# Moving one tap and the history copies of a short convolution from VectorE to ScalarE, in a decoder layer with gated DeltaNet and GLA heads

## The chip, the core and the metric

The kernel runs on one core of one Trainium2 chip. The metric is the device time of one execution in microseconds; for the kernel before, three executions were timed. All arithmetic is float32; large matrix products split each operand into a high and a low part (float32r) and use three matmuls.

## What is computed

One layer of a hybrid decoder for 16 meta tokens, 1024 prompt tokens and 8 samples of 8 tokens. One input projection feeds two groups of heads (gated DeltaNet, "GDN", and GLA); their outputs go through one output projection, a layer norm, a convolutional feed-forward network and a second layer norm. The change lies in the causal convolution of width 4 on the 1536 columns q, k, v of the GDN heads, which follows the projection and comes ahead of a silu:

```python
def causal_conv(x, buf, w):
    width = w.shape[0]
    L = x.shape[1]
    ext = jnp.concatenate([buf.astype(x.dtype), x], axis=1)
    out = ext[:, 0:L] * w[0]
    for i in range(1, width):
        out = out + ext[:, i:i + L] * w[i]
    return out, ext[:, L:]

p = h @ w_in
qkv, new_conv = causal_conv(qkv_pre, conv_buf, gdn_conv_w)
qkv = jax.nn.silu(qkv)
```

The last three rows of the input of each sequence (`new_conv`) are an output too.

## The kernel before

Features lie on the 128 partitions, tokens along the free dimension. There are 1152 positions (48 empty ones, the meta tokens, the prompt, the samples), worked on in three blocks of 384 (`BLK`); the first block leaves out its 48 empty positions in the projections (336 columns).

Phase A, the first half, treats one block after the other. `block(b, order)` emits its parts in the sequence of the string `ORDER[b]`: `k` is the projection, convolution and silu of one of eight feature tiles of q and k, `v` the same for one of four tiles of v, `q`, `V`, `d`, `g` are other projections, `n` norms and the set-up of the GDN heads, `a` and `b` steps of the GLA heads. So `conv_qkv` is called 12 times for each block, 36 times in all. What is emitted is then put in order by a scheduler with its own estimates, engine by engine; instructions of different parts, and of neighbouring blocks, stand mixed on each engine, and each engine works its list strictly in that order. Other work than the convolution may therefore stand elsewhere when the convolution's instructions change.

A projection: SyncE loads 128 x 512 pieces of weights (`wraw`, two for each feature tile), ScalarE copies them to the high part `wwhi` (L212), GpSimd (POOL in the profile) subtracts to get the low part `wwlo` (L213), TensorE does 24 matmuls (L231 to L233) into one of two PSUM banks `mm`. The next projection but one can only start when the bank has been read.

`conv_qkv` then builds the tile `u` (one of two buffers): three history columns, then the block's columns. VectorE copies the history in (L340) and, for blocks 0 and 1, the last three columns out to `hist` for the next block (L345); ScalarE copies the projection from PSUM to `u` (L344). The convolution is four VectorE instructions on `u` into the output tile `o` (named `kq` or `v` in the profile): one product (L371), then three multiply-adds (L373). In block 2 the last 64 columns are the samples, which have a history each; the four taps are done separately for 320 and 64 columns, and L358 and L359 copy the final rows into `ce`, which TensorE turns for the output. ScalarE then makes the sigmoid from three passes (`e`, L329 to L331) and GpSimd multiplies (L375).

Two other stretches matter below. The set-up of the GDN heads inverts a triangular matrix for all chunks by some 60 short dependent VectorE instructions on `lw` and `t` (L558, L560), followed by two transposes (L565, L566); TensorE's L577 needs the first of them. The output projection of blocks 0 and 1 (`out_proj`, matmuls on `mhi` and `mlo`, its sum in `zo` by VectorE at L1111, the low parts `mlo` at L1098) has no dependence on block 2, and the scheduler places it among block 2's work. Phase C, the second half, is the feed-forward network (tiles `up`, `dn`).

Of the kernel before, what the change touches and what calls it, by code (L numbers as in the profile page):

```python
# [46 lines left out]
def hymba_step_kernel(  # L47
# [26 lines left out]
    # tiles in use until the end of the mixers, away from those that the first layer norm's result will cover  # L74
# [3 lines left out]
    def load_x(i):  # L78
        """rows of token tile i (48 empty positions, meta tokens, prompt, samples)."""
# [54 lines left out]
    # ones where two tokens share a chunk (or sample) and the first is not after the second  # L134
# [30 lines left out]
    # per-feature parameters, one row of 128 per feature tile, turned by the tensor engine  # L165
# [44 lines left out]
    def split(raw, hi, lo):  # L210
        """raw = hi + lo, both exact in float32r"""
        act.activation(out=hi, in_=raw, func=AF.Copy)  # L212
        pool.tensor_tensor(out=lo, in0=raw, in1=hi.bitcast(F32), op=ALU.subtract)  # L213

    def stage(src, a, order=(0, 1)):
        """weights [128, a, 1024 / a] as a list of a pairs (hi, lo)"""
        res = {}
        for h in order:
            raw, hi, lo = halves(1, "w")
            v = lambda t: t.rearrange("p (a c) -> p a c", a=a // 2)  # L220
            sp.dma_start(out=v(raw), in_=src[:, h * a // 2:(h + 1) * a // 2])
            split(raw, hi, lo)
            res[h] = [(v(hi)[:, k], v(lo)[:, k]) for k in range(a // 2)]
        return res[0] + res[1]
# [4 lines left out]
    def mm3(ps, lh, rh, first, last):  # L229
        """ps += lh^T rh with both operands as (hi, lo)."""  # L230
# [4 lines left out]
    def layer_norm_rows(small, t, m, src):  # L235
        """t[:m] = (src - mean) * rsqrt(var + eps), rows are tokens; src is a list of two halves."""
# [12 lines left out]
    # =====================================================================  # L249
    # phase A: input projection and both mixers, in three blocks of 384 positions  # L250
    # (48 empty positions, 16 meta tokens, 1024 prompt tokens, 64 sample tokens)
    # =====================================================================
# [23 lines left out]
    def ln_tile(i, hl):  # L276
        """input layer norm of token tile i, turned to features x tokens, to DRAM (and to hi + lo)."""
# [24 lines left out]
    def load_h(b):  # L302
        """normalised input of block b, features x tokens, as hi + lo."""
# [22 lines left out]
    def sigmoid(y, lo=0):  # L326
        """1 / (1 + exp(-y)) = exp(-log(1 + exp(-y)))"""
# [6 lines left out]
    def conv_qkv(b, h, f, o):  # L334
        """projection, causal convolution and silu of feature tile f of q | k | v."""
# [4 lines left out]
        dve.tensor_copy(out=u[:, 0:3], in_=hist[:, f])  # L340
        if b == 0:
            dve.memset(u[:, 3:3 + NPAD], 0.0)
        if b < 2:
            act.activation(out=u[:, 3 + lo:3 + BLK], in_=ps[:, lo:BLK], func=AF.Copy)  # L344
            dve.tensor_copy(out=hist[:, f], in_=u[:, BLK:BLK + 3])  # L345
            parts = [(o, lambda i: u[:, i:i + BLK])]
        else:
# [10 lines left out]
            dve.tensor_copy(out=ce[:, 0:3], in_=u[:, 320:323])  # L358
            dve.tensor_copy(out=ce[:, 3:27].rearrange("p (s i) -> p s i", i=3), in_=us[:, :, 8:11])  # L359
# [9 lines left out]
        tap = lambda i: par[:, TAP + 12 * i + f:TAP + 12 * i + f + 1]  # L369
        for dst, at in parts:  # L370
            dve.tensor_scalar(out=dst, in0=at(0), scalar1=tap(0), scalar2=None, op0=ALU.mult)  # L371
            for i in range(1, 4):
# [18 lines left out]
    def small_in(b, h, out):  # L391
        """decay and step size of the eight GDN heads, tokens on rows; low-rank gate of GLA.

        X: Hb, Hk, Gk, GL - Hk, ln beta, GL of the three token tiles (the first four filled by small_norm)."""
# [17 lines left out]
        # log1p(e) = 2 atanh(e / (2 + e)), e = exp(-|x|)  # L412
# [32 lines left out]
    def small_norm(b, G, X, pss):  # L445
        """norms of k and q folded into the decay exponents, per token and head; rows to DRAM and columns."""
# [18 lines left out]
        # per chunk, the token of head B on partitions 0-63 and that of head A on 64-127  # L465
# [26 lines left out]
    def rms_out(b, hb, po, bank, tmp, tot, scale, g_col, sg, feat):  # L492
        """po (two feature tiles x 192 tokens) normalised per head, gated, written out for the output projection."""
# [14 lines left out]
    def gdn_setup(b, kqs, col, out):  # L508
        """la: decayed k k^T (strict part used) and q k^T of all pairs and chunks, transposed, rows swapped;
        xf: inverses of I + M, M the strict part."""  # L510
# [40 lines left out]
        # column j of the inverse takes the place of column j of -L once that has been used  # L551
# [10 lines left out]
        # xf: X = [[X11, 0], [-X22 M21 X11, X22]] of every chunk, turned  # L562
# [40 lines left out]
    def q_decayed(b, p, kq):  # L603
        """q e^G of pair p, norms folded, in the place of q."""
# [6 lines left out]
    def gdn_batch(b, p, hb, kq, v, col, gln, gls, la, xf, sv, sam, mq):  # L611
        """three chunks of a pair: U's first part into sv, [state | output] operators into mq."""
# [5 lines left out]
        # v and k with tokens on partitions (head B 0-63, head A 64-127)  # L618
# [13 lines left out]
        # w = beta y, (I + M beta) y = [v | e^G k]  # L632
# [13 lines left out]
        # [gl I - Wk^T kd | q e^G - (A Wk)^T]  # L646
# [10 lines left out]
        if s3:  # L657
            for r, ri in halves_:
                pe.matmul(ps[ri, 320:384], wkb[r, 2], la[p][r, 1, 320:384], start=True, stop=True)
            # (in tiles that the previous block's pairs have left)  # L660
# [25 lines left out]
    def gdn_scan(b, g, hb, mqs, sv, sv2, sam, sg):  # L686
        """recurrence over three chunks of two pairs; sv2 takes the next state (None at the end of the block)."""
# [19 lines left out]
        if b == 2 and hb == 1:  # L707
            if g == 0:
                sts = [wk2.tile([128, 8, 64], F32, tag="t2", name="st", bufs=2) for _ in range(4)]
            else:  # L710
                # (in tiles that the GLA heads have left)
# [82 lines left out]
    def mix_gla(b, P, gq, gk, gkl, sgs):  # L794
# [11 lines left out]
        # 16 x the cumulated log decay of each chunk  # L806
# [9 lines left out]
        # k e^{b_last - b}, tokens on partitions  # L816
# [20 lines left out]
        # keys against the end of their 16-block and of their 4-block  # L837
# [18 lines left out]
        def scores(ps, k, n0, n, q):  # L856
            """keys of n chunks against the queries q of each, rows of the two heads swapped."""
# [166 lines left out]
    def block(b, order):  # L1024
        """emits block b; order gives its parts: s small_in, q GLA q and k, V GLA v, k GDN q and k, n norms and
        setup, v GDN v, d GDN gates, g GLA gates, l next block's layer norm, a / b steps of the GLA mixers."""
# [55 lines left out]
    # =====================================================================  # L1082
    # phase B: output projection and first layer norm
    # =====================================================================
    def out_proj(b, zs=None):
        """residual + output projection of block b, features x tokens, to DRAM or to the tile zs."""
# [5 lines left out]
        # the GLA heads are done before the GDN heads  # L1092
# [29 lines left out]
    # per-feature parameters of the FFN: the samples' earlier rows, three taps, bias  # L1122
# [21 lines left out]
    def ln1(i, z=None):  # L1144
        """first layer norm of token tile i, turned to features x tokens as hi + lo."""
# [38 lines left out]
    # =====================================================================  # L1184
    # phase C: convolutional FFN, features on partitions
    # =====================================================================
    # (of the meta tokens only the last two count on, as the convolution's first rows)
# [60 lines left out]
    for j in range(NFF):  # L1248
# [6 lines left out]
        # the sum over two feature blocks goes on between the steps of the next two, and after the last  # L1255
# [7 lines left out]
        if j == 0:  # L1263
            # the banks and the rest of the memory change hands with the first two feature tiles on their way
# [91 lines left out]
```

## Time and profile before

| | us |
|---|---|
| median of three executions | 1785.52 |
| lowest, highest | 1781.99, 1792.48 |
| span of the profiled execution | 1796.3 |
| in it: TensorE busy | 1657.2 (92%) |
| VectorE busy | 1063.3 (59%) |
| GpSimd busy | 873.2 (49%) |
| ScalarE busy | 742.1 (41%) |

The span runs from the first to the last instruction of one profiled execution; no other time of that execution was taken, and its span is 10.8 us above the median of the timed ones. A group row names line, engine, operation, output and inputs, shapes and count; behind the bar stand the busy time of the group in us and the mean duration of one in ns, then the idle time of the engine just ahead of them. In the answers on one line of the code, three numbers are the shortest, median and longest duration in ns. A wait row gives the total in us, the times, and the longest. "Chain" is the work that ended last, followed back from the last instruction to what released it.

### The profile page before, as it was taken

What the parts mean: (1) busy time and instruction counts of PE and PEld (TensorE: products, weight loads), DVE (VectorE), ACT (ScalarE), POOL (GpSimd) and SP (SyncE); (2) the same over time, 40 slices, a digit from 0 to 9 for tenths busy, and PEclk for the clock granted to TensorE, in tenths of its full rate; (3) what the DMA queues carried; (4) which work ended last, traced back from release to release, by engine and by line L of the source; (5) the groups of instructions that cost most, each with busy time, mean ns of one, the idle gap of its engine ahead of it and who ended that gap; (6) DMA issues with size and microseconds to landing.
All of it is one profiled execution on the core that took longest, in us unless ns stands there. A gap on an engine that the chain in (4) does not pass through costs nothing.

```text
span 1796.3 us, 30948 instructions
## 1 busy us (share of the span) xinstructions
PE 1657.2 (92%) x11939; PEld 1521.1 (85%) x11939; DVE 1063.3 (59%) x2083; ACT 742.1 (41%) x1457; POOL 873.2 (49%) x908
## 2 busy tenths in 40 slices
PE   5788799989889998899988999999999999999997
PEld 4677577878677777778878999999999999999996
DVE  7939867696887788962265374443434443434345
ACT  4555544456644556442254433333233323332332
POOL 4756636666555557553354443433334333433336
PEclk9989899989989999798998999999999999999999
DMA  5346313435423224535461111111111111111112
GB/s 147 92 131 164 104 51 89 123 101 136 113 68 89 76 64 117 154 97 139 118 198 42 54 48 42 48 42 48 42 47 44 42 48 42 48 42 48 37 60 100
DMA packets 229504, 148.06 MB, mean 82 GB/s; under 512 B 22251, under 2 KB 222173, under 8 KB 229357
## 3 DMA queue, kind: packets, MB, share of 16 engines
q1 hardware_dynamic: 229357, 146.09, 29.1%
q8 instruction: 94, 1.54, 0.4%
q14 instruction: 53, 0.43, 0.1%
HBM read 124.09 MB, written 21.95 MB: 81 GB/s over the span
## 4 chain that ended last, share of the span: by engine, by line
PE 64%; DVE 19%; DMA 5%; issue 4%; POOL 4%; ACT 3%; SPq 1%; POOLq 0%; ACTq 0%; DVEq 0%
PE up L231 9%; PE up L233 9%; PE up L232 9%; PE dn L233 5%; PE dn L231 5%; PE dn L232 5%; PE mm L232 3%; PE mm L233 3%; PE mm L231 3%; DVE kq L373 2%; DVE lw L560 2%; DVE t L558 2%; DVE qm L886 1%; DVE v L373 1%; DMA mraw<-mixd 1%
## 5 line engine op out<-in xcount | busy, mean ns | idle before, releaser
L213 POOL TENSOR_TENSOR wwlo<-wraw,wwhi 128x512 fp32r<-128x512 f32 x304 | 404.2, 1334 | 520.5 <-ACT wwhi L212 479.9
L212 ACT ACTIVATE wwhi<-wraw 128x512 fp32r<-128x512 f32 x304 | 189.6, 626 | 351.4 <-PE up L232 194.6
L1243 DVE TENSOR_TENSOR acc<-acc,dn 128x364 f32<-128x364 f32 (+1 forms) x216 | 112.3, 531 | 375.7 <-PE dn L233 372.2
L231 PE MATMUL up<-h1hi,wwhi 128*128 128x352 f32 (+2 forms) x1008 | 333.0, 331 | 0.0
L232 PE MATMUL up<-h1lo,wwhi 128*128 128x352 f32 (+2 forms) x1008 | 332.1, 330 | 0.0
L233 PE MATMUL up<-h1hi,wwlo 128*128 128x352 f32 (+2 forms) x1008 | 331.1, 329 | 0.0
L233 PE MATMUL mm<-hhi,wwlo 128*128 128x384 f32 (+1 forms) x576 | 202.5, 353 | 16.6 <-POOL wwlo L213 16.6
L231 PE MATMUL mm<-hhi,wwhi 128*128 128x384 f32 (+1 forms) x576 | 202.2, 351 | 16.7 <-ACT u L344 8.5
L232 PE MATMUL mm<-hlo,wwhi 128*128 128x384 f32 (+1 forms) x576 | 198.3, 344 | 0.0
L232 PEld LDWEIGHTS up<-h1lo,wwhi 128*128 128x128 f32 x1008 | 190.0, 189 | 0.6
L233 PEld LDWEIGHTS up<-h1hi,wwlo 128*128 128x128 f32 x1008 | 189.9, 188 | 0.1
L231 PEld LDWEIGHTS up<-h1hi,wwhi 128*128 128x128 f32 x1008 | 189.6, 188 | 0.2
L232 PE MATMUL dn<-glo,dwh 128*128 128x364 f32 (+1 forms) x480 | 157.4, 328 | 0.0
L231 PE MATMUL dn<-ghi,dwh 128*128 128x364 f32 (+1 forms) x480 | 155.7, 328 | 0.4 <-ACT dwh L212 0.3
L233 PE MATMUL dn<-ghi,dwl 128*128 128x364 f32 (+1 forms) x480 | 151.1, 328 | 0.1
L233 PEld LDWEIGHTS mm<-hhi,wwlo 128*128 128x128 f32 x576 | 112.7, 196 | 27.7 <-POOL wwlo L213 24.3
L231 PEld LDWEIGHTS mm<-hhi,wwhi 128*128 128x128 f32 x576 | 113.5, 197 | 26.1 <-ACT u L344 10.2
L1204 ACT ACTIVATE u<-up 128x352 f32<-128x352 f32 x84 | 38.8, 462 | 194.7 <-PE up L233 193.3
L232 PEld LDWEIGHTS mm<-hlo,wwhi 128*128 128x128 f32 x576 | 113.1, 196 | 2.6 <-issue 1.4
L213 POOL TENSOR_TENSOR dwl<-draw,dwh 128x512 fp32r<-128x512 f32 x40 | 74.5, 1864 | 52.1 <-ACT dwh L212 52.1
L1216 DVE SCALAR_TENSOR_TENSOR y<-u,fpar,y 128x1104 f32<-128x1104 f32 x44 | 94.5, 2148 | 1.1
L231 PEld LDWEIGHTS dn<-ghi,dwh 128*128 128x128 f32 x480 | 90.1, 188 | 0.9 <-ACT dwh L212 0.5
(413 smaller groups left out, 3541.0 us busy)
## 6 DMA issues: line engine op xcount, KB each, us to landing
wraw<-in_w_in_dram SPq DMA_DIRECT2D x168, 256.0 KB
wraw<-in_w_up_dram SPq DMA_DIRECT2D x88, 256.0 KB
wraw<-in_w_out_dram SPq DMA_DIRECT2D x48, 256.0 KB
draw<-in_w_down_dram SPq DMA_DIRECT2D x44, 256.0 KB
hd<-xt SPq DMA_DIRECT2D x9, 512.0 KB
la<-gd SPq DMA_DIRECT2D x24, 192.0 KB
out_dram<-z SPq DMA_DIRECT2D x8, 512.0 KB
xt<-in_x_prompt_dram SPq DMA_DIRECT2D x7, 512.0 KB
```

The lines of the kernel that those rows point to most:

```text
L212: act.activation(out=hi, in_=raw, func=AF.Copy)
L213: pool.tensor_tensor(out=lo, in0=raw, in1=hi.bitcast(F32), op=ALU.subtract)
L231: pe.matmul(ps, lh[0], rh[0], start=first, stop=False)
L232: pe.matmul(ps, lh[0], rh[1], start=False, stop=False)
L233: pe.matmul(ps, lh[1], rh[0], start=False, stop=last)
L373: dve.scalar_tensor_tensor(out=dst, in0=at(i), scalar=tap(i), in1=dst, op0=ALU.mult, op1=ALU.add)
L558: dve.tensor_tensor(out=tv, in0=bc(lw[:, j + 1:32, j:j + 1], 128, n, j), in1=bc(lw[:, j:j + 1, 0:j], 128, n, j), op=ALU.mult)
L560: dve.tensor_tensor(out=lw[:, j + 1:32, 0:j], in0=lw[:, j + 1:32, 0:j], in1=tv, op=ALU.add)
L886: dve.tensor_tensor(out=dst[:, :, off:off + r - c0], in0=v[:, :, c0:r], in1=bc(v[:, :, cr:cr + 1], 128, nn, r - c0), op=ALU.subtract)
L1204: act.activation(out=u[:, t0:t0 + n], in_=ps[:, 0:n], func=AF.Copy)
L1216: dve.scalar_tensor_tensor(out=y[:, 0:1104], in0=u[:, 2:1106], scalar=fpar[:, TAPF + 88 + f:TAPF + 89 + f], in1=y[:, 0:1104], op0=ALU.mult ...
L1243: dve.tensor_tensor(out=acc[:, o, c], in0=acc[:, o, c], in1=ps[:, 0:n], op=ALU.add)
```

## The change

ScalarE takes over the copies of the history columns (L340, L345, L358, L359). The tap of the newest token, which needs no history, becomes a scaled copy by ScalarE straight from PSUM into `o`, behind its copy to `u`; VectorE keeps the three other taps as multiply-adds, in falling order. In block 0 VectorE also clears the 48 empty columns of `o`. Behind this place the lines of the changed file are three higher (L371 and L373 of before have become L373, the ScalarE pass, and L376, the multiply-adds; L558, L560, L565, L1111 are L561, L563, L568, L1114).

```diff
-        dve.tensor_copy(out=u[:, 0:3], in_=hist[:, f])
+        act.activation(out=u[:, 0:3], in_=hist[:, f], func=AF.Copy)
...
             act.activation(out=u[:, 3 + lo:3 + BLK], in_=ps[:, lo:BLK], func=AF.Copy)
-            dve.tensor_copy(out=hist[:, f], in_=u[:, BLK:BLK + 3])
+            act.activation(out=hist[:, f], in_=u[:, BLK:BLK + 3], func=AF.Copy)
...
-            dve.tensor_copy(out=ce[:, 0:3], in_=u[:, 320:323])
-            dve.tensor_copy(out=ce[:, 3:27].rearrange("p (s i) -> p s i", i=3), in_=us[:, :, 8:11])
+            act.activation(out=ce[:, 0:3], in_=u[:, 320:323], func=AF.Copy)
+            act.activation(out=ce[:, 3:27].rearrange("p (s i) -> p s i", i=3), in_=us[:, :, 8:11], func=AF.Copy)
...
+        if b == 0:
+            dve.memset(o[:, 0:NPAD], 0.0)
+        act.activation(out=o[:, lo:], in_=ps[:, lo:BLK], func=AF.Copy, scale=tap(3))
         for dst, at in parts:
-            dve.tensor_scalar(out=dst, in0=at(0), scalar1=tap(0), scalar2=None, op0=ALU.mult)
-            for i in range(1, 4):
+            for i in range(2, -1, -1):
                 dve.scalar_tensor_tensor(out=dst, in0=at(i), scalar=tap(i), in1=dst, op0=ALU.mult, op1=ALU.add)
```

The first place is the middle of block 0's k tiles, on VectorE. Before:

```order
L340 COPY u<-hist 128x3
L342 MEMSET u 128x48
L345 COPY hist<-u 128x3
L371 TENSOR_SCALAR kq<-u,par 128x384
L373 SCALAR_TENSOR_TENSOR kq<-u,par,kq 128x384 x2
L440 COPY G<-ms 128x24
L441 COPY X<-ms 128x3x8
L373 SCALAR_TENSOR_TENSOR kq<-u,par,kq 128x384
```

Now, in the same place on VectorE (`G` and `X` are small tiles of the decays, emitted by another part):

```order
L342 MEMSET u 128x48
L434 MEMSET g 48x8
L376 SCALAR_TENSOR_TENSOR kq<-u,par,kq 128x384 x3
L443 COPY G<-ms 128x24
L342 MEMSET u 128x48
L444 COPY X<-ms 128x3x8
```

Two copies and the product have gone from VectorE; the three multiply-adds and the clearing of 48 columns stay.

On ScalarE a piece of the same stretch read before:

```order
L344 ACTIVATE u<-mm 128x336
L329 ACTIVATE e<-kq 128x384
L330 ACTIVATE e<-e 128x384
L212 ACTIVATE wwhi<-wraw 128x512
L331 ACTIVATE e<-e 128x384
```

And it reads now:

```order
L330 ACTIVATE e<-e 128x384
L212 ACTIVATE wwhi<-wraw 128x512
L344 ACTIVATE u<-mm 128x336
L373 ACTIVATE kq<-mm,par 128x336
L331 ACTIVATE e<-e 128x384
L329 ACTIVATE e<-kq 128x384
L340 ACTIVATE u<-hist 128x3
L345 ACTIVATE hist<-u 128x3
L212 ACTIVATE wwhi<-wraw 128x512
```

The scaled copy stands right behind the copy to `u`; the copy into the history columns stands right behind the first pass of an earlier tile's sigmoid.

The second place is the end of block 2's triangular inversion on VectorE. Before:

```order
L1111 SCALAR_TENSOR_TENSOR zo<-zo,ms 128x322
L558 TENSOR_TENSOR t_6969<-lw 128x84
L560 TENSOR_TENSOR lw<-lw,t_6969 128x3x28
L558 TENSOR_TENSOR t_6969<-lw 128x58
L561 MEMSET lw 128x32
L560 TENSOR_TENSOR lw<-lw,t_6969 128x2x29
L558 TENSOR_TENSOR t_6969<-lw 128x30
L560 TENSOR_TENSOR lw<-lw,t_6969 128x30
L565 STREAM_TRANSPOSE xn<-lw 128x32x32
L566 STREAM_TRANSPOSE xf<-lw 128x32x32
```

Now, on the same engine:

```order
L1101 TENSOR_TENSOR mlo<-mraw,mhi 128x322
L563 TENSOR_TENSOR lw<-lw,t_6973 128x3x28
L561 TENSOR_TENSOR t_6973<-lw 128x58
L564 MEMSET lw 128x32
L563 TENSOR_TENSOR lw<-lw,t_6973 128x2x29
L561 TENSOR_TENSOR t_6973<-lw 128x30
L563 TENSOR_TENSOR lw<-lw,t_6973 128x30
L568 STREAM_TRANSPOSE xn<-lw 128x32x32
L569 STREAM_TRANSPOSE xf<-lw 128x32x32
L1114 SCALAR_TENSOR_TENSOR zo<-zo,mm 128x322
```

Before, sums of block 0's output projection (`zo`) stood among the inversion's last steps; now it is only the preparation of its operands (`mlo`), and the first `zo` follows the inversion. On TensorE, 110 matmuls of that projection stood ahead of the third L577, and 38 now do.

## The prediction

> **What bounds the kernel now.** I read the page's engine shares and the chain of work that ended last, then the busy time in stretches, then the chain and the timeline of one stretch with convolutions. First the chain's shares by engine and the stretches (microseconds from the span's start; TensorE, weight loads, VectorE, ScalarE, GpSimd busy, then the granted clock):
>
> ```profile
> PE 64%; DVE 19%; DMA 5%; issue 4%; POOL 4%; ACT 3%; SPq 1%; POOLq 0%; ACTq 0%; DVEq 0%
> ...
> 0.00:215.00 215.00, 163.65 (x1125) 137.04 (x1127) 166.98 (x347) 108.50 (x230) 127.54 (x125) 0.94 0.47 127
> 215.00:430.00 215.00, 197.54 (x1618) 167.52 (x1613) 158.55 (x382) 107.51 (x222) 131.95 (x151) 0.94 0.36 93
> 430.00:640.00 210.00, 185.97 (x1686) 152.48 (x1686) 169.80 (x424) 111.99 (x250) 114.91 (x123) 0.93 0.36 96
> 640.00:870.00 230.00, 206.12 (x1967) 177.11 (x1963) 160.40 (x383) 103.17 (x225) 130.53 (x140) 0.89 0.43 118
> 870.00:1000.00 130.00, 117.45 (x833) 109.69 (x830) 63.88 (x125) 57.08 (x104) 53.83 (x52) 0.92 0.40 116
> 1000.00:1796.30 796.30, 786.47 (x4732) 777.27 (x4730) 343.73 (x425) 253.86 (x429) 314.44 (x321) 1.00 0.16 49
> ```
>
> From 1000 us on TensorE is busy 99% at full clock; the change has no instruction there. Up to 870 us VectorE is busy 655.7 of 870 us (75%), ScalarE 431.2 (50%), GpSimd 504.9. TensorE looks busier, 753 us, but its matmuls overlap, as two neighbours show (start, duration):
>
> ```profile
> 758.45 0.32 PE L231 MATMUL mm<-mhi,wwhi 128*128 128x322 f32 x1
> 758.60 0.31 PE L232 MATMUL mm<-mlo,wwhi 128*128 128x322 f32 x1
> ```
>
> One starts 0.15 us behind the other and is booked 0.31, so a lone matmul counts double. TensorE is thus no floor that far up. Where the convolutions of block 0 stand, the chain is VectorE's (44 to 70 us, share by line):
>
> ```profile
> by line: DVE kq L373 39.4%; issue 12.1%; DVE W L423 10.4%; DVE kq L371 9.0%; DVE bcm L808 7.7%; POOL wwlo L213 4.8%; DVE W L420 4.4%; DVE hist L345 4.3%; DVE u L340 4.0%; POOL kq L375 2.0%; DVE g L818 1.8%; DVE u L342 0.6%; DVE W L419 0.5%;
> ```
>
> Why a copy of three columns shows up there at all is told by VectorE's and GpSimd's timelines in that stretch:
>
> ```profile
> 59.14 1.48 POOL L213 TENSOR_TENSOR wwlo<-wraw,wwhi 128x512 fp32r<-128x512 f32 x1 [2.19 <-ACT wwhi L212]
> 60.59 1.33 POOL L375 TENSOR_TENSOR kq<-kq,e 128x384 f32<-128x384 f32 x1
> 61.88 2.65 POOL L213 TENSOR_TENSOR wwlo<-wraw,wwhi 128x512 fp32r<-128x512 f32 x2
> ...
> 59.53 1.51 DVE L373 SCALAR_TENSOR_TENSOR kq<-u,par,kq 128x384 f32<-128x384 f32 x1
> 61.07 0.87 DVE L340 COPY u<-hist 128x3 f32<-128x3 f32 x1
> 61.89 0.10 DVE L342 MEMSET u<- 128x48 f32 x1
> 61.91 0.11 DVE L345 COPY hist<-u 128x3 f32<-128x3 f32 x1
> 61.94 1.45 DVE L371 TENSOR_SCALAR kq<-u,par 128x384 f32<-128x384 f32 x1
> ```
>
> A VectorE instruction on SBUF that meets a running GpSimd instruction ends only after it: the copy L340 until 61.94, as L375 ends at 61.92; the product L371 until 63.39, behind one of the two L213 that end at 64.53. Such waits are booked as busy.
>
> **What is removed.** VectorE's groups, total and mean; then the shortest, median and longest of some:
>
> ```profile
> L371 DVE TENSOR_SCALAR kq<-u,par 128x384 f32<-128x384 f32 (+2 forms) x32 | 15.4, 488 | 0.1
> L345 DVE COPY hist<-u 128x3 f32<-128x3 f32 x24 | 13.6, 567 | 7.9 <-ACT u L344 7.9
> L340 DVE COPY u<-hist 128x3 f32<-128x3 f32 x36 | 12.9, 357 | 0.5
> L371 DVE TENSOR_SCALAR v<-u,par 128x384 f32<-128x384 f32 (+2 forms) x16 | 9.5, 592 | 0.1
> L358 DVE COPY ce<-u 128x3 f32<-128x3 f32 x12 | 6.4, 531 | 0.6 <-ACT u L348 0.6
> L359 DVE COPY ce<-u 128x24 f32<-128x24 f32 x12 | 3.6, 297 | 0.0
> L342 DVE MEMSET u<- 128x48 f32 x12 | 1.2, 98 | 0.0
> ...
> L340 DVE COPY u<-hist x36: 154/170/1221, 4.6 to 660.4; 128x3 f32<-128x3 f32 x36
> L345 DVE COPY hist<-u x24: 108/364/1248, 38.7 to 402.8; 128x3 f32<-128x3 f32 x24
> L371 DVE TENSOR_SCALAR kq<-u,par x32: 241/406/1449, 39.8 to 609.8; 128x384 f32<-128x384 f32 x16, 128x320 f32<-128x320 f32 x8, 128x64 f32<-128x64 f32 x8
> ```
>
> As booked, 15.4 + 13.6 + 12.9 + 9.5 + 6.4 + 3.6 = 61.4 us go; 12 new clearings like L342 add 1.2, so 60 us net. Without the waits on GpSimd it is less: 36 x 0.154 (L340) + 24 x 0.108 (L345) + 36 x 0.406 (L371 on 384 or 320 columns, at the median) + 12 x 0.241 (on 64) + 24 x about 0.15 (L358, L359, priced as L340) = 29 us, 28 net. The truth lies between, since a wait that a removed instruction bore may fall to the next one.
>
> How much of it is on the path? The chain's 19% of VectorE is 341 us, practically all ahead of 870 us, of 655.7 busy there: half. So the relief is worth 14 us (half of 28) to 30 us (half of 60). I take 23, slightly above the middle: at 59 to 64 us each VectorE instruction of the convolution stands beside its own GpSimd instruction, so one fewer is nearly one wait fewer.
>
> A rule speaks for the low end. The Trainium skill, page "SBUF — State Buffer", section "Who interferes with whom", says that GpSimd and VectorE lock a shared port pair for a whole instruction, and that an instruction of VectorE with two SBUF inputs meets that lock too. The three multiply-adds left are of that kind, and L373's 1.51 us at 59.53, beside L213, agrees. By that rule alone the waits pass on to them, the relief would be 14 us, and the time some 1777 by the rest of the sum below; the row of one wait for each instruction keeps me higher.
>
> **What is added on ScalarE.** There the nearest rows are the copies from PSUM of the same width and the narrowest copy from SBUF:
>
> ```profile
> L344 ACT ACTIVATE u<-mm 128x384 f32<-128x384 f32 x12 | 5.7, 472 | 0.0
> L344 ACT ACTIVATE u<-mm 128x336 f32<-128x336 f32 x12 | 5.2, 432 | 0.0
> L815 ACT ACTIVATE gl<-bcm 128x6 f32<-128x6 f32 x4 | 0.8, 195 | 0.0
> ```
>
> 36 scaled copies: 12 x 0.432 + 24 x 0.472 = 16.5 us; 84 narrow copies (36 L340, 24 L345, 24 L358 and L359) x 0.195 = 16.4 us. Together 33 us, ScalarE to 53% of the first 870 us. What waits:
>
> ```profile
> ACT e L329 <- DVE kq L373: 52.3, 19, 5.4
> ACT e L329 <- DVE v L373: 30.4, 10, 6.1
> POOL wwlo L213 <- ACT wwhi L212: 130.3, 67, 7.1
> PE mm L233 <- POOL wwlo L213: 17.4, 27, 2.2
> PE mm L231 <- ACT u L344: 8.5, 5, 3.6
> ```
>
> ScalarE already stands 82.7 us still for last taps. The copy L340 now stands right behind such an L329, and u's buffer comes free with a last tap, so it should find its wait over. Queued behind ScalarE's new work are the splits L212, and behind them L213 and TensorE. The chain's 3% of ScalarE is 54 us of 742 busy, so 33 us more should cost about 7% of it, 2.4 us. Its bounds are 0 (all in its 82.7 us of standing still) and 33 (all on the path).
>
> The scaled copy also holds the `mm` bank 0.43 to 0.47 us longer. TensorE waited for that bank 5 times; five such waits grow by 2.3 us, all 36 would by 17. I take 3: with 24 matmuls of 0.15 us, 3.7 us, between a bank's end and the next need, most are covered, and if ScalarE falls back by more than that the cover is gone. In a convolution for which VectorE stands ready nothing is won or lost: 0.43 to 0.47 of scaled copy replaces 0.41 of L371. The falling order of taps costs nothing, the instructions being the same. Loads and GpSimd's instructions are unchanged in number; only their places move.
>
> **Sum.** -23 + 2.4 + 3 = -18 us. On the profiled span 1796.3 that is 1778; the span stands 10.8 above the median of the runs, so the time comes to 1785.5 - 18 = 1768 us. From the first two bounds alone: -14 + 5 = -9 to -30 + 5 = -25. What is late next is TensorE's and GpSimd's part of phase A, which the chain then goes through.
>
> **Rivals.** About 0.5% (9 us) is what a measurement of this kernel can tell from no change.
>
> *Absorbed.* The relief falls where TensorE has queued work anyway (90% to 92% booked from 215 to 430 and 640 to 870 us), and only block 0's stretch profits: its quarter of VectorE's time up to 870 (167 of 656 us) times 23 is 6 us, less block 0's third of the added costs (2 us): 1782. For it speaks TensorE's 64% of the chain, against it the overlapped booking.
>
> *The inversion comes due too early.* In block 2 the end of the inversion and L577 stood so:
>
> ```profile
> 753.80 2.04 DVE L565 STREAM_TRANSPOSE xn<-lw 128x1024 f32<-128x1024 f32 x1
> ...
> 758.84 1.71 PE L577 MATMUL gd<-xn,la 32*32 32x32 f32 x96
> ```
>
> Only 3.0 us lay between the transpose's end and L577. The new order puts 72 output-projection matmuls fewer ahead of L577: 72 x 0.15 = 11 us. If VectorE's inversion isn't earlier by at least 11 - 3 = 8 us there, TensorE stands still before it, up to 11 us, and those matmuls come later. Gain left -18 + 11 = -7: 1778, no measurable change.
>
> *Slower: ScalarE feeds the weights late.* The new 33 us stand between splits in an engine that works in order; each delays L212, L213 and the next projection. With the relief at its low 14 and all 33 on that path the time is 1785.5 - 14 + 33 = 1804; at two thirds, 1794. It decides from 14/33, 42% of the added work on the path. For it: GpSimd's 130.3 us of waiting for L212. Against: TensorE's own waits for L213 are only 17.4 us, and ScalarE is idle half the time.
>
> *More than the sum.* If the taps end earlier, ScalarE's 82.7 us of standing still shrink too, and splits and loads move up. The whole 30 us with no added cost, and 7 us (about a tenth of 82.7) more, give 1749.
>
> **How the numbers follow.** Forecast (gain of 9 to 30 us) 0.48; more than the sum 0.07; absorbed 0.20; inversion early 0.10; slower 0.15. Faster by over 0.5%: 0.48 + 0.07 = 0.55. Within 0.5%: 0.20 + 0.10 = 0.30. Slower: 0.15. The range 1748 to 1795 reaches to the larger gain and to two thirds of ScalarE's work on the path, and leaves out perhaps 0.18. The forecast's own range is 1755 to 1776.
>
> **What would show it.** VectorE's booked time up to the end of phase A down by 28 to 60 us, and the multiply-adds' mean (0.75 us for kq, 0.85 for v) not above before by much; if it rises, the waits were handed on. ScalarE's new copies at 0.43 to 0.47 and 0.2 us. ScalarE's waits for last taps below 82.7. TensorE's waits for the `mm` bank not above 12 us, and for L213 about 17. No gap of several us ahead of the third L577. The feed-forward network from its first `up` on as long as before. I am wrong if VectorE is relieved and phase A doesn't end earlier, or if the copies on ScalarE stand still for u's buffer and carry the splits with them.

## The result, and the profile after

The changed kernel takes 1800.53 us (median of 7 runs, 1796.54 to 1805.82) against 1789.65 us for the kernel before (7 runs, 1781.99 to 1793.25): a ratio of 1.0061 with a 95% interval of 1.0039 to 1.0083. It is slower by 0.6%, where 1768 us were forecast. The profiled execution of after has a span of 1804.1 us. Its stretches, to be laid beside those of before (same columns: TensorE, weight loads, VectorE, ScalarE, GpSimd busy, then the granted clock):

```profile
0.00:215.00 215.00, 166.93 (x1128) 143.53 (x1130) 159.57 (x321) 116.73 (x269) 127.62 (x129) 0.90 0.47 127
215.00:430.00 215.00, 194.86 (x1579) 165.23 (x1578) 135.88 (x340) 108.54 (x243) 123.96 (x141) 0.91 0.34 89
430.00:640.00 210.00, 182.76 (x1629) 150.53 (x1628) 165.57 (x384) 116.83 (x278) 116.78 (x124) 0.90 0.36 95
640.00:870.00 230.00, 207.31 (x2017) 179.75 (x2017) 151.85 (x364) 113.73 (x254) 137.23 (x144) 0.91 0.44 119
870.00:1000.00 130.00, 112.85 (x823) 104.00 (x821) 65.09 (x131) 52.74 (x99) 53.80 (x48) 0.92 0.40 116
```

VectorE has been relieved: 612.9 us up to 870, where it had 655.7. ScalarE has 455.8 instead of 431.2. But TensorE has started fewer matmuls in the second and third stretch (1579 and 1629, before 1618 and 1686): it has done less by 640 us although VectorE had less to do. The first matmul of the feed-forward network, in before and in after, shows where the whole difference lies:

```profile
990.98 0.33 PE L231 MATMUL up<-h1hi,wwhi 128*128 128x352 f32 x1
```

```profile
998.76 0.33 PE L231 MATMUL up<-h1hi,wwhi 128*128 128x352 f32 x1
```

From there to the end both take 805.3 us (1796.3 - 991.0 and 1804.1 - 998.8). So 7.8 us are lost ahead of it. What TensorE did up to that matmul, in the same columns, before and then after:

```profile
0.00:990.98 990.98, 861.71 (x7155) 734.82 (x7156) 716.32 (x1656) 482.46 (x1020) 555.71 (x582) 0.93 0.40 110
```

```profile
0.00:998.76 998.76, 863.46 (x7156) 741.79 (x7156) 676.75 (x1536) 507.55 (x1140) 559.39 (x582) 0.91 0.40 109
```

TensorE stands idle for 129.3 us before and 135.3 after: 6.0 of the 7.8 us are waits, the rest is busy time. The changed groups, by line (total and mean, then the idle time ahead of them):

```profile
L376 DVE SCALAR_TENSOR_TENSOR kq<-u,par,kq 128x384 f32<-128x384 f32 (+2 forms) x96 | 71.7, 762 | 11.9 <-ACT kq L373 10.7
...
L376 DVE SCALAR_TENSOR_TENSOR v<-u,par,v 128x384 f32<-128x384 f32 (+2 forms) x48 | 37.7, 788 | 12.1 <-ACT v L373 11.5
```

The means of the multiply-adds are not much above before's (750 and 849 ns then, so 762 is a little more and 788 less): the waits on GpSimd were not handed on to them. What is new is the last column: 22.2 us in which VectorE stands still for the scaled copy. That copy, and the copy of three columns (shortest, median, longest):

```profile
L373 ACT ACTIVATE kq<-mm,par x24: 525/572/588, 39.5 to 607.6; 128x384 f32<-128x384 f32 x16, 128x336 f32<-128x336 f32 x8
...
L340 ACT ACTIVATE u<-hist x36: 186/188/206, 2.8 to 703.5; 128x3 f32<-128x3 f32 x36
```

And the waits of ScalarE for last taps, then those of TensorE up to 1000 us for the inversion, the next block's input and the operands behind it (total, times, longest); first after:

```profile
ACT e L329 <- DVE kq L376: 31.0, 15, 5.0
...
ACT e L329 <- DVE v L376: 17.5, 7, 4.3
```

```profile
PE mm L231 <- ACT mhi L1100: 8.1, 5, 3.1
PE gd L580 <- DVE xn L568: 7.5, 2, 5.8
...
PE ms L232 <- DVE hlo L315: 5.0, 2, 4.2
PE gd L640 <- DVE la L633: 4.8, 4, 3.1
PE mm L231 <- ACT v L373: 4.0, 2, 2.7
...
PE mm L231 <- ACT kq L373: 0.6, 1, 0.6
```

The same list of before:

```profile
PE gd L577 <- issue: 6.2, 1, 6.2
...
PE mm L231 <- ACT mhi L1097: 2.4, 3, 1.6
...
PE ms L232 <- DVE hlo L315: 1.8, 2, 1.5
...
PE gd L577 <- DVE xn L565: 1.3, 1, 1.3
```

ScalarE's waits fell from 82.7 to 48.5 us: the taps do end sooner. Some of TensorE's waits of before are gone too (8.5 us for L344's reading of the bank, 7.2 of 8.2 for `svg`, a tile of the GLA heads). Yet it now waits where it did not wait, or waits longer, and the largest of these places hold no instruction that the change touched: `hlo` is the low part of the next block's input, `la` an operand of the GDN heads, `mhi` one of the output projection. For the scaled copies, which now free the `mm` bank, it waits 4.6 us.

### The profile page after: what moved, and what is told of

The parts are those of the page before. It is cut to its first block, busy times and chain, and to the rows that moved or that the text cites. A ratio compares the mean times of both kernels' runs of the same rounds, so it can differ in the third digit from the quotient of the medians.

```text
span 1804.1 us, 30960 instructions
## 1 busy us (share of the span) xinstructions
PE 1659.0 (92%) x11939; PEld 1528.1 (85%) x11939; DVE 1023.5 (57%) x1963; ACT 767.5 (43%) x1577; POOL 876.1 (49%) x908
## 5 line engine op out<-in xcount | busy, mean ns | idle before, releaser
L213 POOL TENSOR_TENSOR wwlo<-wraw,wwhi 128x512 fp32r<-128x512 f32 x304 | 403.5, 1333 | 542.6 <-ACT wwhi L212 494.7
L212 ACT ACTIVATE wwhi<-wraw 128x512 fp32r<-128x512 f32 x304 | 190.0, 627 | 360.3 <-PE up L232 196.1
L213 POOL TENSOR_TENSOR dwl<-draw,dwh 128x512 fp32r<-128x512 f32 x40 | 74.1, 1852 | 52.4 <-ACT dwh L212 52.4
```

## Experiments

My theory after this comparison: the relief is real, and the order of all the other instructions, made anew by the scheduler, costs more than it brings. The rivals: ScalarE's added work costs it (and the order is only a consequence), or TensorE's clock, granted at 0.948 after and 0.958 before.

### Work and order taken apart

To run one kernel's instructions in the other's order, a table at the end of the kernel tells the scheduler for each engine which instruction comes behind which:

```diff
+    for engine, deltas in table.items():
+        n, last = 0, None
...
+            if last is not None:
+                tc.add_manual_dep(i, last.name, nosync(), reason="order")
+            last = i
```

Instructions that only one of the two kernels has are placed by the scheduler; all others stand on every engine in the order of the other kernel. The scaled copy reads `u` here:

```diff
-        act.activation(out=o[:, lo:], in_=ps[:, lo:BLK], func=AF.Copy, scale=tap(3))
         for dst, at in parts:
+            act.activation(out=dst if b else dst[:, lo:], in_=at(3) if b else at(3)[:, lo:], func=AF.Copy, scale=tap(3))
```

Old work, new order. 

> The instructions of before, each engine's in the order of after (the 96 VectorE instructions that after hasn't stand where the scheduler puts them). Theory 'order' (the relief of VectorE is real, but the new order of all the other instructions costs more): slower than before by more than after is, about after plus the forecast relief, 1800 + 18 = 1818 us, at least 1800. Theory 'work' (ScalarE's added 33 us and the longer hold of the mm bank cost it, the order is only a consequence): within 0.5% of before, about 1790 us. Theory 'clock' (TensorE's granted clock falls where the engines are denser): the clock stays at before's 0.958 and the time at about 1790 us.

Measured: 1823.27 us, ratio 1.0189 (1.0157 to 1.0220). Not one instruction of the change is in it, and it is 34 us slower than before. (The 96 instructions that the new order doesn't know stand where the scheduler put them; what part of the 34 us is theirs isn't known.)

New work, old order. 

> The changed kernel's instructions, with every other instruction on every engine in the order of before. The scaled copy reads u instead of the PSUM bank (in block 2 in two pieces, 320 and 64 columns), as the old order can't be kept with the bank held that long; so the bank's longer hold is left out. Theory 'order': faster than before by the forecast's sum without its 3 us for the bank, 1790 - 21 = 1769 us, and certainly not slower. Theory 'work': slower than before, about 1797 to 1800 us. Theory 'clock': the granted clock falls to 0.948 here too, and the time is at or above before's 1790 us.

Measured: 1782.87 us, ratio 0.9967 (0.9946 to 0.9989). The change, kept in the old order, is a small gain, of 6 us where the theory had 21.

New work, new order, with the same stand-in. 

> The changed kernel's instructions in the order of after, with the scaled copy from u as in the run in the old order: what that stand-in itself is worth. Theory 'order': as after, 1800 us, within 5 us (bank's hold worth at most the 3 us of the forecast). Theory 'work', if the bank is what costs: back at about 1790 us or below; if the engine time is what costs: 1800 us.

Measured: 1805.08 us, ratio 1.0079 (1.0050 to 1.0109), as after within the intervals. The stand-in is worth nothing that can be seen, so the bank's longer hold isn't the cause. The new order costs 34 us with the old work and 20 us (1.0079 - 0.9967, of 1790) with the new. In the new order the change's work gains 1.1%, 20 us (1.0189 against 1.0079), more than in the old one: the relief is there in both.

The clock is not cleared by this. In the new order it was lower: 0.943 to 0.948 in the six runs with the old work, where the 22 runs of before beside them had 0.954 to 0.968, and 0.949 to 0.953 with the new work, where the old order had 0.954 to 0.962. So it went down with the order, also where no work was moved. But it can't be the whole cause. The profiled executions of the last two runs had nearly the same clock, 0.954 in the old order and 0.953 in the new, and took 1791.78 and 1803.94 us. Up to the first `up` their engines were busy as follows, old order first:

```profile
0.00:984.71 984.71, 862.48 (x7156) 737.40 (x7156) 678.36 (x1536) 509.70 (x1152) 551.09 (x582) 0.92 0.40 110
```

```profile
0.00:996.88 996.88, 859.12 (x7155) 739.32 (x7156) 680.19 (x1536) 512.16 (x1152) 555.37 (x582) 0.92 0.40 109
```

TensorE stands idle for 122.2 us in the old order and 137.8 in the new. In this pair of executions, at one clock, the new order thus costs 12 us, and all of it is waits. The medians of the two kernels lie 22 us apart; whether the clock makes the other 10 us, and what lowers it, isn't shown.

### Is any new order worse?

Half of the change in its own order:

```diff
-        dve.tensor_copy(out=u[:, 0:3], in_=hist[:, f])
+        act.activation(out=u[:, 0:3], in_=hist[:, f], func=AF.Copy)
...
-            dve.tensor_copy(out=hist[:, f], in_=u[:, BLK:BLK + 3])
+            act.activation(out=hist[:, f], in_=u[:, BLK:BLK + 3], func=AF.Copy)
```

(and the two copies to `ce` likewise). 

> Half of the change: the copies of the history columns (L340, L345, L358, L359) on ScalarE, the newest token's tap left where it was on VectorE; the scheduler orders it anew. Booked relief of VectorE 36.5 us, half of the low and high bound on the path 6 to 18 us, ScalarE +16 us. By the forecast's way of counting 1790 - 11 + 1 = 1780 us. Theory 'work': slower than before by half of after's loss, about 1795 us. Theory 'order': the time isn't given by the work; anything from 1770 to 1800 us, and its loss or gain sits where the projections and the inversion's matmuls change places.

Measured: 1798.30 us, ratio 1.0055 (1.0035 to 1.0076). The same code in the old order: 

> The narrow copies (L340, L345, L358, L359) on ScalarE, the tap on VectorE, in the order of before; the same code in the scheduler's own order was 0.55% slower than before. Relief 36.5 us booked x 17.7/48.5 = 13; ScalarE 84 x 0.2 = 17 us at about a half, 8. Theory 'order': 1790 - 5 = 1785 us, well under its own order's 1800. Theory 'work': 1800 us as there.

Measured: 1784.69 us, ratio 0.9971 (0.9953 to 0.9989). The order alone is again 0.84%, 15 us, and here at nearly one clock: 0.956 to 0.961 in the new order, 0.957 to 0.964 in the old.

A change that only takes work from VectorE:

```diff
-        dve.tensor_copy(out=u[:, 0:3], in_=hist[:, f])
         if b == 0:
-            dve.memset(u[:, 3:3 + NPAD], 0.0)
+            dve.memset(u[:, 0:3 + NPAD], 0.0)
+        else:
+            dve.tensor_copy(out=u[:, 0:3], in_=hist[:, f])
```

> How much the scheduler's order alone may move the time: before, with a change that only takes work away (block 0's clearing of u covers its first three columns, so the 12 copies L340 of block 0 and the clearing of hist are gone, 4 us booked on VectorE), ordered anew by the scheduler: 1323 lines of TensorE's order differ. Theory 'any new order is a throw of the dice around before's': off by more than the 1.5 us that the work is worth, between 1780 and 1805 us. Theory 'the order after is bad for a reason of its own (ScalarE's copies)': 1786 to 1790 us.

Measured: 1791.28 us, ratio 0.9999 (0.9980 to 1.0017). This doesn't answer the question, since the order is hardly a new one. By the traces, with tile names without their buffer numbers, TensorE's list of 11,939 instructions differs from before's in 18 lines (taken out and put in counted together), after's in 3344; the 1323 lines expected aren't found there. What it shows is that 12 copies fewer in before's order are worth nothing that can be seen. The scheduler's order was worse than the old one in each of the three kernels with work moved to ScalarE that ran in both: the copies (1646 lines differ), the change without L340, below (3176), and the whole change. Whether any order so far from before's would be as bad, whatever the change, no run tests. Why the scheduler chooses these is open as well: its estimates weren't changed in any run.

### Where the new order loses

Three cuts first: the new order up to a point, the old one from there on, always with the new work (and the scaled copy from `u`). The order table is then after's list up to an instruction, followed by what is left of before's list.

Up to the first inversion's L577. 

> The changed kernel's instructions (scaled copy from u) in the order of after up to the first inversion's first matmul (L577, block 0, about 200 us), and from there on what remains in the order of before. The run wholly in the old order took 1783, the one wholly in the new order 1805 us. Theory 'order, one spot after another': at this point the new order stood 3.3 us ahead (199.8 against 203.1 us) with as many matmuls done, so 1780 us. Theory 'the new order is worse all along': a quarter of the 22 us, 1788 us.

Measured: 1783.22 us, ratio 0.9961 (0.9945 to 0.9977).

Up to the second inversion's. 

> As before, with the new order kept up to the second inversion's first matmul (block 1, about 518 us), then the old one. There the new order stood 1.8 us ahead, but with 58 matmuls fewer done (58 x 0.15 = 9 us): by that count 1783 + 7 = 1790 us. It holds the waits at 225 to 250 us for la and at 450 to 500 us for the next block's input. If these cost nothing in the end, 1783 us or less.

Measured: 1798.19 us, ratio 1.0047 (1.0031 to 1.0063).

Up to the third. 

> As before, with the new order kept up to the third inversion's first matmul (block 2, about 755 us), then the old one. There the new order stood 10 us behind and 72 matmuls (11 us) fewer were done: 1783 + 21 = 1804 us, all of the new order's loss, which would place 14 of the 22 us between the second and the third inversion. If the loss lies in the output projection behind it instead, 1790 us.

Measured: 1807.46 us, ratio 1.0095 (1.0079 to 1.0111). Nothing is lost up to 200 us, 15 us between the first and the second inversion, 9 us between the second and the third, and nothing behind it. In the profiles of the three, TensorE stands idle ahead of the first `up` for 118.0, 131.3 and 141.0 us, so most of both losses are waits. Two cuts more divide the 15:

> The changed kernel's instructions in the order of after until the first convolution of block 1 (its L344, about 240 us), from there on in the old order. With the cut at the first inversion (about 200 us) the time was 0.9961 of before, with the cut at the second (about 518 us) 1.0047. Where the mixing right behind the first inversion costs it (waits for la of 4 us, that L344 11 us later): 0.996 + 11/1790 = 1.002, 1793 us. Where that is caught up again by the old order behind it: 0.996 to 0.998, 1785 us.

Measured: 1789.90 us, ratio 0.9995 (0.9976 to 1.0013): some 6 us by 240 us, though its interval just touches that of the cut at 200.

> As the run before, cut behind the last convolution of block 1 (its L344, about 414 us against 392 in the old order). All of the delay is then there, the late load of block 2's input inside the inversion (450 to 500 us) is not taken over. If the delay of the convolutions is the loss: 1.0047 as with the cut at the second inversion, 1798 us. If the waits for hlo inside the inversion are: 0.998 to 1.000, 1788 us.

Measured: 1793.82 us, ratio 1.0030 (1.0015 to 1.0044): 6 us more by 414 us. The last 3 up to the second inversion, where the waits for `hlo` lie, are within the intervals. The loss isn't in one spot.

The first spot can be read on ScalarE, right behind the first inversion, in the runs with the first and the second cut: up to 200 us both have the new order, up to 518 us only the second. First the run that is in the old order from 200 us on (`rb` is an operand of the GDN heads, copied from PSUM by L631):

```profile
213.28 0.33 ACT L631 ACTIVATE rb<-gd 128x192 f32<-128x192 f32 x1
213.55 0.63 ACT L212 ACTIVATE wwhi<-wraw 128x512 fp32r<-128x512 f32 x1
214.09 0.31 ACT L631 ACTIVATE rb<-gd 128x192 f32<-128x192 f32 x1
```

Then the run that stays in the new order:

```profile
212.21 0.33 ACT L631 ACTIVATE rb<-gd 128x192 f32<-128x192 f32 x1
216.57 0.63 ACT L212 ACTIVATE wwhi<-wraw 128x512 fp32r<-128x512 f32 x1 [4.03 <-DMA wraw<-in_w_in_dram]
217.22 1.05 ACT L684 ACTIVATE mq<-la 64x384 f32<-64x384 f32 x2
218.19 1.13 ACT L212 ACTIVATE wwhi<-wraw 128x512 fp32r<-128x512 f32 x2
219.23 0.31 ACT L631 ACTIVATE rb<-gd 128x192 f32<-128x192 f32 x1
```

In the new order a split of weights that have not arrived stands ahead of the second `rb`. ScalarE waits 4 us for the load, `rb` comes at 219.2 instead of 214.1, VectorE's L632 and L633 behind it, and TensorE stands still:

```profile
220.33 1.29 PE L640 MATMUL gd<-rb,xf 64*64 64x128 f32 x9 [3.09 <-DVE la L633]
```

By the next convolution the delay is 11 us (its copy to `u`, old order first):

```profile
228.88 0.47 ACT L344 ACTIVATE u<-mm 128x384 f32<-128x384 f32 x1
```

```profile
239.51 0.47 ACT L344 ACTIVATE u<-mm 128x384 f32<-128x384 f32 x1
```

Later the block's last convolution is late (392.0 in the old order, 414.4 in the new), and the next block's input with it. In the old order TensorE meets this input ahead of the inversion:

```profile
451.00 0.36 PE L232 MATMUL ms<-hlo,wsh 128*32 128x384 f32 x1 [0.69 <-DVE hlo L315]
```

In the new order the subtraction L315 stands on VectorE among the inversion's steps, two of which are shown with it, and TensorE waits for it:

```profile
473.44 1.36 DVE L853 TENSOR_TENSOR g<-bcm 128x384 f32<-128x384 f32 x1
474.72 1.10 DVE L563 TENSOR_TENSOR lw<-lw,t 128x150 f32<-128x150 f32 x1
475.75 1.34 DVE L315 TENSOR_TENSOR hlo<-hraw,hhi 128x384 fp32r<-128x384 f32 x1
477.02 0.32 DVE L561 TENSOR_TENSOR t<-lw 128x168 f32<-128x168 f32 x1
```

```profile
477.15 0.53 PE L232 MATMUL ms<-hlo,wsh 128*32 128x384 f32 x1 [4.24 <-DVE hlo L315]
```

### The terms of the work, in the old order

Relief alone (this kernel leaves out a part of the convolution, so that VectorE is relieved and nobody has more to do):

```diff
-            dve.tensor_copy(out=hist[:, f], in_=u[:, BLK:BLK + 3])
...
-            pe.transpose(pt[0:27, 0:128], ce, ident)
+            pe.transpose(pt[0:27, 0:128], u[:, 320:347], ident)
...
-            dve.tensor_scalar(out=dst, in0=at(0), scalar1=tap(0), scalar2=None, op0=ALU.mult)
...
-                dve.scalar_tensor_tensor(out=dst, in0=at(i), scalar=tap(i), in1=dst, op0=ALU.mult, op1=ALU.add)
+                dve.scalar_tensor_tensor(out=dst, in0=at(i), scalar=tap(i), in1=at(0) if i == 1 else dst, op0=ALU.mult,
+                                         op1=ALU.add)
```

> VectorE's relief with nothing put on ScalarE, in the order of before: L371's product, the copies to hist (L345) and to ce (L358, L359) are left out (the first multiply-add takes u's oldest column set unscaled, the transpose reads u): 48.5 us booked of the 61.4 that the change removes. Theory 'relief as forecast, ScalarE takes it back': 48.5/61.4 of 23 = 18 us, 1770 us. Theory 'absorbed' (in a fixed order TensorE meets other waits anyway): a gain like the whole change's 5 us or little more, 1780 to 1784 us.

Measured: 1772.61 us, ratio 0.9901 (0.9884 to 0.9917): 17.7 us.

ScalarE's work alone:

```diff
+        spare = wk2.tile([128, 380], F32, tag="spare", name="spare", bufs=1)
+        act.activation(out=spare[:, 377:380], in_=hist[:, f], func=AF.Copy)
...
+            act.activation(out=spare[:, 0:n], in_=u[:, 3 + lo:3 + lo + n], func=AF.Copy, scale=tap(3))
```

> The other half of the change: before's instructions in before's order, and on ScalarE as many copies more as the change puts there (36 scaled ones of 332 to 380 columns, in block 2 in two pieces, and 84 narrow ones), written to a spare tile that nobody reads. So ScalarE has the added work and VectorE all of its own. The forecast's 2.4 us: 1790 + 2 = 1792 us. Theory 'ScalarE takes the relief back': the relief alone gave 17.7 us for 48.5 booked, 22 for the change's 61.4, and the whole change in the old order gave 5.9; so the added work costs 16 us, 1806 us. Above 1815 (all 33 on the path) is not expected.

Measured: 1793.66 us, ratio 1.0022 (1.0002 to 1.0042): 4 us, not 16. The two together:

> The relief alone (as e8, the same instructions left out) and ScalarE's added copies to a spare tile (as e9) in one kernel, in the order of before: nobody waits for the added copies. Additive: 1790 - 17.7 + 4 = 1776 us. If ScalarE's occupied time weighs more once VectorE is relieved: as the whole change in the old order, 1783 us or more. If additive, the change's missing 8 us come from waits for ScalarE's copies, not from its time.

Measured: 1774.82 us, ratio 0.9918 (0.9897 to 0.9940): 14.7 us. They add up. So the change's 6 us in the old order, 9 less than this, are not for want of ScalarE's time. (In both of these kernels L340 stays on VectorE; its 12.9 us booked are relief that only the whole change has. So the waits may cost more than 9.) The waits up to 870 us tell the two kernels apart. First the change in the old order (there the scaled copy is L374), ScalarE's and VectorE's waits:

```profile
ACT u L340 <- DVE v L376: 8.5, 4, 3.9
```

```profile
DVE kq L376 <- ACT kq L374: 18.9, 12, 3.6
...
DVE v L376 <- ACT v L374: 8.7, 5, 2.9
```

Then VectorE's in the kernel with relief and ScalarE's work, but no dependence between them (multiply-adds at L375, the copy to `u` at L346):

```profile
DVE kq L375 <- ACT u L346: 4.6, 4, 1.6
...
DVE v L375 <- ACT u L346: 2.0, 3, 0.8
```

VectorE waits 27.6 us for the scaled copy where it waited 6.6 for the copy to `u`, and ScalarE itself stands 8.5 us in L340, for a buffer of `u` that a last tap of `v` still reads.

The tap alone on ScalarE (from `u`), the narrow copies on VectorE: 

> The newest token's tap as a scaled copy (from u), the narrow copies on VectorE, in the order of before. Relief 24.9 us booked x 17.7/48.5 = 9; ScalarE's 36 scaled copies, about 20 us, at a half: 10. So 1790 us, no difference. If the scaled copy is cheap where it stands (ScalarE then waits less for last taps), 1783 us.

Measured: 1781.30 us, ratio 0.9955 (0.9936 to 0.9974).

All of the change but L340, in its own order and in the old one:

```diff
-        act.activation(out=u[:, 0:3], in_=hist[:, f], func=AF.Copy)
+        dve.tensor_copy(out=u[:, 0:3], in_=hist[:, f])
```

> The change without its copy L340 (u's first three columns stay on VectorE, where they can be written before the projection is there), all else moved, the scheduler's own order. Theory 'own order is worse': between 1.000 and 1.008 of before, as the change and the copies alone in their own orders. If L340 on ScalarE is what made it bad: below 1790 us.

Measured: 1794.75 us, ratio 1.0025 (1.0008 to 1.0042).

> The same as the run before it (all of the change but L340, which stays on VectorE; scaled copy from u), now in the order of before. Relief and ScalarE's time together gave 0.9918, the whole change in this order 0.9967. If the missing 9 us come from L340's place on ScalarE (u's first columns, and with them the first multiply-add, wait for an engine that works in order): about 0.992 to 0.993, 1777 us. If they come from the multiply-adds' wait for the scaled copy: 0.9955 to 0.997 as with the whole change and with the tap alone, 1783 us.

Measured: 1782.07 us, ratio 0.9938 (0.9918 to 0.9958). Between its two orders lie 0.87%, 16 us. Against the whole change in the old order it gains 0.29%, 5 of the 9 us; since the intervals overlap, that share isn't certain. The waits for the scaled copy are still 21.7 us here:

```profile
DVE kq L376 <- ACT kq L374: 15.2, 11, 2.4
...
DVE v L376 <- ACT v L374: 6.5, 5, 2.7
```

The last run joined the two findings. 

> The change without L340's move, in the order that the earlier cuts favour: after's up to the first inversion (about 200 us), before's from there on. In the old order throughout it took 0.9938 of before; the whole change gained a further 0.0006 by this cut (0.9961 against 0.9967, within their intervals). So 0.993, 1778 us; if the first stretch's gain of 3.3 us at the first inversion lasts, 0.992, 1776 us. Above 0.996 the cut is worth nothing here.

Measured: 1781.10 us, ratio 0.9955 (0.9939 to 0.9971). The cut brings nothing more here. The version without L340 in the old order throughout beats both kernels, by 0.6% of before and some 1.2% of after (0.9938 against 1.0061); the tap alone and this last one cannot be told from it.

## Why the prediction was wrong, point by point

- **Relief of VectorE, 23 us: right.** VectorE's booked time fell by 39.8 us (1063.3 to 1023.5), in the forecast's 28 to 60. Relief alone gave 17.7 us for 48.5 booked, where the forecast's 23 for 61.4 has 18 for the same part. So the low end, 14 us with the waits handed on, did not come. One reading behind it is too wide: that a VectorE instruction which meets a running GpSimd instruction ends only after it. Two of the lines shown for it say otherwise, L342 and L345 at 61.89 and 61.91 us, which took 0.10 and 0.11 us although an L213 is booked from 61.88 on.
- **ScalarE's added time, 2.4 us: about right.** 4 us alone (0.4 to 7.5 by the interval), 3 beside the relief. The scaled copies took 0.572 us instead of the 0.472 taken from the plain copy of 384 columns, and the narrow ones 0.19 as forecast. The scaled copy takes its scale from a column, by a pointer. The Trainium skill, page "ScalarE: Activation LUTs", section "What ACT_TABLE_LOAD costs", gives about 93 ns for each such operand, and the difference of 0.1 us in the trace agrees. For 36 copies that difference is 3.6 us of busy time. The forecast's 0.43 to 0.47 us for the scaled copy was a sign that did not come true.
- **The `mm` bank, 3 us: at most that.** TensorE's waits for the bank's last reader were 4.6 us, 8.5 before, and the stand-in that frees the bank earlier changed nothing beyond the intervals.
- **Costed at nothing, and not nothing: the waits for ScalarE's copies.** The prediction had L340 find "its wait over", and nothing lost where VectorE stands ready. In the old order L340 stood 8.5 us, and the multiply-adds 27.6. Work and relief without these waits give 14.7 us, the change 6: 9 us, of which L340 may be 5.
- **The step that failed: the sum stops at the convolution's own instructions.** It says that loads and GpSimd's instructions are unchanged, "only their places move", and prices no move but that of 72 matmuls at the third inversion. The moves of instructions that the change doesn't touch cost 20 us with the new work and 34 us with the old. The sum, corrected: relief and ScalarE's time 14.7 gained, 9 lost in new waits, 20 lost by the order, so 14 us slower in the kernel with the stand-in; after itself is slower by 11. The sum has no term for the clock either, and in the 20 us is whatever the lower clock of the new order costs: 0.949 is the median over after's runs, and 0.961 over the runs of before whose clock is on record.
- **The rival on the inversion** had the right kind of cause and the wrong place. TensorE did not stand still ahead of the third L577. Of its 7.5 us of waiting for this transpose 5.8 lie in block 0, which are booked as 6.2 us of "issue" before. The transpose in block 2 ended later, not earlier:

```profile
755.82 1.98 DVE L568 STREAM_TRANSPOSE xn<-lw 128x1024 f32<-128x1024 f32 x1
...
761.08 1.71 PE L580 MATMUL gd<-xn,la 32*32 32x32 f32 x96
```

- **The rival that ended slower** (ScalarE feeds the weights late, 1794 to 1804) gave the right time for a reason that fell: the same added time on ScalarE costs 4 us in the old order. What holds up `rb` behind the first inversion is where L212 stands, not how long ScalarE is busy.
- **The two other rivals** fell. *Absorbed* has a relief of 6 us, and the relief alone gave 17.7. *More than the sum* has 37, and that run, with nothing put on ScalarE, stayed below 18 for 48.5 of the 61.4 us.
- **Signs that came true:** means of the multiply-adds, ScalarE's waits for last taps, no gap ahead of the third L577, the length of the second half. TensorE's waits for L213 fell from 17.4 to 14.5. The prediction named the case in which it is wrong, "VectorE is relieved and phase A doesn't end earlier", and that is what happened.

Open is why the scheduler's orders with work on ScalarE are worse, whether any order as far from before's would be, what lowers the clock in the new order, and which move between the second and the third inversion loses the 9 us there: TensorE's waits for `mhi` grew from 2.4 to 8.1 us, but no run took that place by itself.

## What to carry to other kernels

Where a scheduler places the instructions, a changed line has two effects, its own work and the new places of everything else, and here the second was three times the first (20 us lost, 6 gained). Before such a change is judged, run the new work in the old order and the old work in the new one; the four times say which of the two to mend. When work moves to another engine, count besides its time who then waits for it, and what stands behind it in that engine's queue while it waits for a buffer.

## What the runs showed of the hardware

A scaled copy of 128 x 384 from PSUM with the scale in a column takes 0.572 us on ScalarE, the plain one 0.472. VectorE's copies of three columns had a mean of 0.357 us (0.154 to 1.221) and the same copies 0.188 (0.186 to 0.206) on ScalarE: there the wait on a running GpSimd instruction is absent. TensorE's granted clock was lower in the new order with the same instructions (0.943 to 0.948 against 0.954 to 0.968), and within one kernel a lower clock went with a longer time: of the twelve runs with ScalarE's added work in the old order, the four at 0.949 to 0.952 took 1799 to 1806 us, the eight at 0.956 to 0.962 took 1786 to 1797. From these runs a clock lower by 1% is worth some 10 us here, by estimate, so two kernels are best compared in executions with the same clock.
